# Moving 64 partition-group copies of the first mixer from ScalarE and VectorE to DMA, and some of its side products one main block later

## The chip, the cores and the metric

One core of one Trainium2 chip runs the whole program in a single launch. The core has five engines, each with its own instruction stream: TensorE (PE, matmuls into PSUM), VectorE (DVE), ScalarE (ACT), GpSimd (POOL) and SyncE (SP, which here issues DMAs). The metric is the device time of one launch in microseconds, the median of the runs.

## The reference

Two transformer blocks in fp32 over a sequence of 256 tokens, width 1024, batch 1. The first block puts 16 meta tokens ahead of the sequence (272 rows); the change touches only its mixer:

```python
hn = rmsnorm(h, norm1_g)
u, q, k, v, g_ssm, g_att = split(hn @ w_in)           # widths 512, 512, 512, 512, 1024, 1024
y_ssm = s5_mixer(u, ...)      # 32 groups of 16 channels, each a 64-dim complex state; scan over time
                              # y = gelu(Re(C s) + d * u);  y * sigmoid(y @ glu_w + glu_b)
q, k = rmsnorm per head ...
o = diff_attention(q, k, v, lam, slopes)               # 4 heads, softmax minus lam * softmax, ALiBi
y_att = rmsnorm(o, subln_g) * (1 - lam_init)
mixed = sigmoid(g_ssm) * (y_ssm @ w_ssm_out) + sigmoid(g_att) * (y_att @ w_att_out)
h = h + mixed @ w_o
h = h + conv_glu_ffn(rmsnorm(h, norm2_g), ...)
```

The second block (RG-LRU, HGRN2 and block-sparse attention side by side, then a squared-ReLU FFN and a final norm) is the same before and after.

## The kernel before

**Main work.** All large products keep fp32 accuracy by splitting both factors into a high and a low part of the faster fp32r type: `ah`/`al` for activations, `whi`/`wlo` for weights. A weight chunk of 1 MB is loaded by an SP DMA into one of two `raw` buffers (L109); ACT then makes `whi` (L133) and DVE makes `wlo` = raw - whi (L134). Half a chunk is a unit, which serves two blocks of 128 output rows (one for the first norm's direct products). A main block is 24 products, hi·hi, hi·lo and lo·hi for each of 8 slices of the contraction, into one of three `mm` PSUM tiles. `blocks()` walks units and blocks: in the first mixer the order is k, q (first norm's part in plain fp32), u (4 blocks), v (4), the 16 gate blocks `tg` (units 8 to 23), and then the output products of attention, the S5 gate, S5 and `w_o`. The next unit's split is issued after each block by `tick()`, up to four units ahead.

**Side work.** The S5 branch and the attention are Python generators. After each main block `bg.step()` advances them, by a budget of estimated DVE time, so that their small instructions are placed between the main blocks. After that a scheduler fixes the order on each engine; on the chip every engine runs its list in order and waits on semaphores. Side products use four `ps` PSUM tiles, and one `pso` tile for the attention's last norm. An instruction on PE that waits for ACT or DVE holds up all PE work behind it.

**The S5 branch.** Its preparation (`s5_prep`) forms small products of B and C (`s5cp`, `s5b`: 32 products), evicts them as `s5ks` (ACT), and copies them into the block-Toeplitz matrix `s5tz`: 16 copies of 32 partitions, each from one group of 32 partitions to another (`move`, L242 on ACT). It transposes `s5bp` by 32 PE transposes into 8 PSUM tiles, evicted as `s5lt` (ACT). When the u blocks are done, `stack()` copies `u` into `us`, 16 copies of 32 partitions x 272, so that time steps lie in partition groups. `s5_main` then goes through four channel tiles `ct`: 8 products with `s5lt`, eviction to `s5wk`, rotation, eight scans and rotation back on DVE (`s5wk`, `s5e`), 12 products with `s5cp` and `s5tz`, and eviction of the result `ys` into `us`. After the second and the fourth tile 16 copies of 32 x 136 bring the result back into `u` (`u<-us`): on ACT after the second (L242), on DVE after the fourth (L247), as the table `UNV = (1,)` says. A gelu (`u<-u`, ACT) and the split `yhl` follow.

**The attention.** The row norms of q and k run as a chain of small DVE instructions on `rw`, then ACT writes `rowt`, which PE spreads over the partitions (`rowt,bs`). Each head makes scores (`kraw,qz`), a softmax on DVE and ACT (`sc`, `sm`), five transposes of `sc`, an eviction to `wt`, and products `wt,vn`. After four heads the same chain on `rw` norms the result, `ya` is formed and split into `oh`/`ol`, the factors of the output product. A weight load on SP waits for the `wlo` that last read its raw buffer, and each engine's queue is served in order.

Of the kernel before, what the change touches and what calls it, by code (L numbers as in the profile page):

```python
# [33 lines left out]
NC = T // 4  # L34
# [19 lines left out]
MIX = "agass"  # L54
UNV, TZV, STV = (1,), (), ()
L_SO, L_O, L_F1, L_M2, L_F2 = 2, 0, 0, 2, 2
# [87 lines left out]


class Bg:


    def __init__(self, b):
        self.b, self.tc, self.tasks, self.ahead = b, b.tc, [], {}  # L150
        self.due = 0.0

    def add(self, gen, ahead=0):
# [4 lines left out]
    def one(self):  # L158
        for g in list(self.tasks):
            try:  # L160
                with self.tc.high_priority(self.ahead[g]) if self.ahead[g] else nullcontext():
                    self.b.side = True
                    next(g)
            except StopIteration:
                self.tasks.remove(g)
            self.b.side = False
# [12 lines left out]
    def finish(self, *gens):  # L179
        for g in gens:  # L180
            while g in self.tasks:
                self.one()


class Build:
    def __init__(self, ctx, tc, I, out, dbg):
        self.ctx, self.tc, self.I, self.out, self.dbg = ctx, tc, I, out, dbg or {}
        nc = self.nc = tc.nc
        self.V, self.A, self.G, self.PE = nc.vector, nc.scalar, nc.gpsimd, nc.tensor
        self.dve, self.side = 0.0, False  # L190
        self.bg = Bg(self)
        self.led = {}
        pool = lambda n, bufs, **k: ctx.enter_context(tc.tile_pool(name=n, bufs=bufs, **k))
        self.const = pool("const", 1)
        self.act_p = pool("act", 1)
        self.pad(self.act_p, 0)
        self.raw_p = pool("raw", 2)
        self.pad(pool("pad1", 1), 1)
        self.spl_p = pool("spl", 4)
        self.tmp_p = pool("tmp", 3)  # L200
        self.mm_p = pool("mm", 3, space=PSUM)
        self.ps_p = pool("ps", 4, space=PSUM)
        self.pso_p = pool("pso", 1, space=PSUM)
        self.dram = pool("dram", 1, space=DRAM)
# [38 lines left out]

    def move(self, o, i, vector):
        if vector:
            self.count(o)
            return self.V.tensor_copy(o, i)  # L247
        return self.cp(o, i)

# [102 lines left out]
    def s5_prep(self):  # L352
# [128 lines left out]
        for n in range(5):  # L481
# [17 lines left out]
            yield  # L499
        self.s5_stage = 1  # L500

        pk = self.ps()
# [11 lines left out]
        yield  # L514

        tz = self.s5_t
        for q in range(4):
            for i in range(4):
                self.move(tz[32 * i:32 * i + 32, :, q, i:4], ks[32 * q:32 * q + 32, :, 0:4 - i], i in TZV)
            yield  # L520

# [16 lines left out]
        for ct in range(2):  # L538
            self.s5_phases(ct)
            yield  # L540

# [43 lines left out]
    def s5_main(self):  # L585
# [7 lines left out]
        for ct in range(4):  # L593
# [38 lines left out]
            if ct % 2 == 1:  # L632
                for q in range(4):
                    for j in range(4):
                        o, i = yb[32 * q:32 * q + 32, ct - 1:ct + 1, j * NC:(j + 1) * NC], ys[32 * j:32 * j + 32, ct - 1:ct + 1, q]
                        self.move(o, i, ct // 2 in UNV)
                    yield
# [113 lines left out]
    def att_norm(self):  # L751
# [11 lines left out]
        self.rows_norm(p, 16, T, 1.0 / 64, eps=EPS * EPS)  # L763
        yield
        self.gk = a.tile([P, 1], F32, name="gk")
# [70 lines left out]
    def att_head(self, h):  # L836
# [26 lines left out]
        for i, (cols, _) in enumerate(rng):  # L863
            self.act(sc[:, 1, cols], sc[:, 1, cols], AF.Copy, scale=sm[:, 3, 2 + i:3 + i])
            self.stt(sc[:, 0, cols], sc[:, 0, cols], sm[:, 3, i:i + 1], sc[:, 1, cols], ALU.mult, ALU.add)
        yield
        p0, p1 = self.ps(), self.ps()
# [9 lines left out]
        self.cp(wt, p1[:, 0:3 * P])  # L877
        yield
        po = self.ps()
# [10 lines left out]
    def att_main(self):  # L890
# [9 lines left out]
        while gens or live:  # L900
            if gens:
                live.append(gens.pop(0))
            for _ in range(3):
                for g in list(live):
                    try:
                        next(g)
                    except StopIteration:
                        live.remove(g)
                yield
        self.show("o", self.o)  # L910
        self.rows_norm(self.pso, 8, TQ, 1.0 / P, mult=2.0 * (1.0 - LAM0))
        yield
        self.oh, self.ol = (a.tile([P, 4, RS], F32R, name=n, tag=t)[:, :, 0:TQ] for n, t in (("oh", "qz0"), ("ol", "qz1")))
# [52 lines left out]
    def blocks(self, ids, ah, al, n, bud=None, whole=None):  # L966

        b = 0
        for u in ids:
# [3 lines left out]
            self.W.used = u  # L973
            for c in range(w[0].shape[2] // P):
                if c < len(begun):
                    o, done = begun[c]
# [13 lines left out]
    def mixer1(self):  # L990
        tc, bg = self.tc, self.bg
        with ExitStack() as es:
# [28 lines left out]
            while self.s5_stage < 1:  # L1021
                bg.one()
            at = bg.add(self.att_main(), A_AT)
# [5 lines left out]
            def stack():  # L1029
                for q in range(4):  # L1030
                    for j in range(4):
                        self.move(self.us[32 * j:32 * j + 32, 0:16 * NC].rearrange("p (c q k) -> p c q k", c=4, q=4)[:, :, q],
                                  self.u[32 * q:32 * q + 32, :, j * NC:(j + 1) * NC], j in STV)
                        if j % 2 == 1:
# [9 lines left out]
            while self.s5_stage < 2:  # L1044
                bg.one()
            tg = self.tg = self.at_p.tile([P, 16, TQ], F32, name="tg", tag="tg")
# [788 lines left out]
```

## Time and profile before

| | before |
|---|---|
| time, median of 3 runs | 726.87 us (726.18 to 729.63) |
| profiled execution's own time | 726.51 us |
| span of the profiled execution | 724.7 us |
| PE busy | 699.3 us (96%) |
| DVE busy | 559.4 us (77%) |
| ACT busy | 437.6 us (60%) |
| POOL busy | 24.3 us (3%) |
| share of the chain that ended last: PE, DVE, ACT | 81%, 9%, 6% |

The span runs from the first to the last instruction of the profiled execution; the 1.8 us between it and that execution's time lie outside. Busy time is the time in which an engine executes; PE's is that of matmuls. The first mixer takes about the first 225 us. A timeline row gives an instruction (or several alike in a row, "x16"), when it starts, how long it takes, and in brackets how long the engine idled before it and which instruction ended that wait.

### The profile page before, as it was taken

How to read it: one execution, taken by the hardware profiler on the slowest of the kernel's cores; microseconds unless marked ns; L12 is line 12 of the kernel's file. 1: busy time of each engine (PE TensorE's matmuls, PEld its weight loads, DVE VectorE, ACT ScalarE, POOL GpSimd, SP SyncE). 2: the span in 40 equal slices, each digit the busy share in tenths (PEclk: the TensorE clock that was granted, in tenths of full speed). 3: DMA queues.
4: the chain of work that ended last, by engine and by line, in shares of the span. 5: the costliest groups of instructions: out<-in, count | busy, mean ns of one | idle time of the engine just before them, and what ended most of it. 6: DMA issues, size and time to landing. Idle time of an engine off the chain costs nothing.

```text
span 724.7 us, 13692 instructions
## 1 busy us (share of the span) xinstructions
PE 699.3 (96%) x5346; PEld 656.6 (91%) x5346; DVE 559.4 (77%) x1267; ACT 437.6 (60%) x813; POOL 24.3 (3%) x74
## 2 busy tenths in 40 slices
PE   8998998999999999999999998999899999999995
PEld 5886897989999999999999998898799999988884
DVE  8996788988989998888656598997778777744543
ACT  7488548655666655555454487779467666633421
POOL 5020000000001000000000300000000000000000
PEclk9999999999999999999999999999999999999999
DMA  7551303135457555445556634332237565555531
GB/s 256 203 184 72 123 35 117 59 117 175 179 181 252 178 198 206 176 175 189 190 167 212 211 139 175 118 117 73 103 117 241 203 214 186 181 213 188 179 112 58
DMA packets 18225, 117.24 MB, mean 162 GB/s; under 512 B 2160, under 2 KB 2416, under 8 KB 5360
## 3 DMA queue, kind: packets, MB, share of 16 engines
q1 hardware_dynamic: 17136, 113.55, 44.9%
q0 software_dynamic: 448, 2.16, 0.9%
q8 instruction: 42, 0.69, 0.4%
q10 hardware_dynamic: 576, 0.65, 0.3%
q14 instruction: 23, 0.19, 0.1%
HBM read 115.30 MB, written 1.05 MB: 161 GB/s over the span
## 4 chain that ended last, share of the span: by engine, by line
PE 81%; DVE 9%; ACT 6%; DMA 2%; issue 1%; SPq 0%; ACTq 0%; DVEq 0%
PE mm L263 72%; PE ps L263 7%; PE ps L259 2%; DVE wlo L134 2%; DVE s5w L217 1%; DMA cst<-in_cst_dram 1%; ACT s5tz L242 1%; ACT whi L133 1%; DVE s5bc L217 1%; ACT us L242 1%; DMA raw<-in_w_up_dram 1%; PE pso L263 1%; DVE s5x L217 1%; DVE s5an L236 1%; ACT u L242 1%
## 5 line engine op out<-in xcount | busy, mean ns | idle before, releaser
L133 ACT ACTIVATE whi<-raw 128x1024 fp32r<-128x1024 f32 (+1 forms) x206 | 215.5, 1051 | 193.2 <-PE mm L263 168.8
L134 DVE TENSOR_TENSOR wlo<-raw,whi 128x1024 fp32r<-128x1024 f32 (+1 forms) x206 | 249.9, 1214 | 103.1 <-ACT whi L133 101.8
L263 PE MATMUL mm<-ah,whi 128*128 128x256 f32 (+2 forms) x992 | 281.2, 284 | 0.4 <-DVE a L217 0.4
L263 PE MATMUL mm<-al,whi 128*128 128x256 f32 (+2 forms) x992 | 279.9, 282 | 0.0
L263 PE MATMUL mm<-ah,wlo 128*128 128x256 f32 (+2 forms) x992 | 279.2, 282 | 0.0
L263 PEld LDWEIGHTS mm<-ah,whi 128*128 128x128 f32 x992 | 187.4, 189 | 2.2 <-issue 1.0
L263 PEld LDWEIGHTS mm<-al,whi 128*128 128x128 f32 x992 | 187.4, 189 | 1.6 <-issue 1.1
L263 PEld LDWEIGHTS mm<-ah,wlo 128*128 128x128 f32 x992 | 187.3, 189 | 0.5 <-issue 0.4
L263 PE MATMUL mm<-whi,f2h 128*128 128x512 f32 x128 | 49.8, 389 | 0.0
L263 PE MATMUL mm<-whi,f2l 128*128 128x512 f32 x128 | 49.8, 389 | 0.0
L263 PE MATMUL mm<-wlo,f2h 128*128 128x512 f32 x128 | 49.8, 389 | 0.0
L263 PE MATMUL mm<-fl,whi 128*128 128x256 f32 x176 | 48.6, 276 | 0.0
L263 PE MATMUL mm<-fh,wlo 128*128 128x256 f32 x176 | 48.6, 276 | 0.0
L263 PE MATMUL mm<-fh,whi 128*128 128x256 f32 x176 | 48.6, 276 | 0.0
L263 PEld LDWEIGHTS mm<-fh,whi 128*128 128x128 f32 x176 | 33.0, 188 | 0.0
L263 PEld LDWEIGHTS mm<-fl,whi 128*128 128x128 f32 x176 | 33.0, 188 | 0.0
L263 PEld LDWEIGHTS mm<-fh,wlo 128*128 128x128 f32 x176 | 33.0, 188 | 0.0
L263 PE MATMUL mm<-hT,whi 128*128 128x272 f32 (+1 forms) x128 | 29.5, 389 | 0.0
L263 PEld LDWEIGHTS mm<-hT,whi 128*128 128x128 f32 x128 | 23.9, 190 | 5.2 <-ACT hT L239 1.3
L263 PEld LDWEIGHTS mm<-whi,f2h 128*128 128x128 f32 x128 | 24.0, 188 | 5.0
L263 PEld LDWEIGHTS mm<-whi,f2l 128*128 128x128 f32 x128 | 24.0, 188 | 5.0
L263 PEld LDWEIGHTS mm<-wlo,f2h 128*128 128x128 f32 x128 | 24.0, 188 | 4.9
(411 smaller groups left out, 1098.9 us busy)
## 6 DMA issues: line engine op xcount, KB each, us to landing
raw<-in_w_ff_dram SPq DMA_DIRECT2D x32, 1024.0 KB, 4.8
raw<-in_w_in_dram SPq DMA_DIRECT2D x24, 1024.0 KB, 4.8
raw<-in_w_up_dram SPq DMA_DIRECT2D x22, 1024.0 KB, 4.8
raw<-in_w_down_dram SPq DMA_DIRECT2D x8, 1024.0 KB, 4.8
whi<-in_w_in_dram SPq DMA_DIRECT2D x8, 512.0 KB, 5.0
raw<-in_w_o_dram SPq DMA_DIRECT2D x4, 1024.0 KB, 4.8
raw<-in_w_out_dram SPq DMA_DIRECT2D x4, 1024.0 KB, 4.8
raw<-in_w_down_dram SPq DMA_DIRECT2D x4, 768.0 KB, 4.4
```

Source lines behind the costliest of these rows:

```text
L133: b.A.activation(out=hi[:, 0:m], in_=raw, func=AF.Copy)
L134: b.V.tensor_tensor(out=lo[:, 0:m], in0=raw, in1=hi[:, 0:m].bitcast(F32), op=ALU.subtract)
L217: return self.V.tensor_tensor(out=o, in0=a, in1=b, op=op)
L236: return self.V.scalar_tensor_tensor(out=o, in0=a, scalar=s, in1=b, op0=op0, op1=op1)
L242: return self.A.activation(out=o, in_=i, func=AF.Copy)
L259: return self.PE.transpose(out=o, in_=i, identity=self.ident[0:k, 0:k])
L263: return self.PE.matmul(out=o, lhsT=l, rhs=r, start=start, stop=stop)
```

## The change

The three kinds of copy between partition groups become DMAs that SP issues, from SBUF to SBUF; the table `UNV` and the choice between ACT and DVE go. The 16 copies into `s5tz` are also issued later, after the transposes and the first phases of `s5_prep`. And a generator can now yield a mark, `LATER`, at six places: it is then not advanced again until the next main block has begun (`nblk`), whatever the budget. The marks stand before the `s5cp,s5b` products and before the `s5bp` transposes, after the row norm of q and k, in each head before the transposes of `sc` and before the products with `wt`, and after the last row norm. Where the program must have a generator's result, `force()` lifts the hold.

```diff
-UNV, TZV, STV = (1,), (), ()
...
+LATER = object()
...
     def one(self):
         for g in list(self.tasks):
+            if self.held.get(g) == self.b.nblk:
+                continue
             try:
...
-                    next(g)
+                    if next(g) is LATER:
+                        self.held[g] = self.b.nblk
...
-                self.one()
+                self.force()
+
+    def force(self):
+        self.held.clear()
+        self.one()
...
-    def move(self, o, i, vector):
-        if vector:
-            self.count(o)
-            return self.V.tensor_copy(o, i)
-        return self.cp(o, i)
+    def move(self, o, i):
+
+        self.nc.sync.dma_start(out=o, in_=i)
...
         self.s5_stage = 1
+        yield LATER
...
-        tz = self.s5_t
-        for q in range(4):
-            for i in range(4):
-                self.move(tz[32 * i:32 * i + 32, :, q, i:4], ks[32 * q:32 * q + 32, :, 0:4 - i], i in TZV)
-            yield
+        yield LATER
...
         for ct in range(2):
             self.s5_phases(ct)
+            yield
+
+        tz = self.s5_t
+        for q in range(4):
+            for i in range(4):
+                self.move(tz[32 * i:32 * i + 32, :, q, i:4], ks[32 * q:32 * q + 32, :, 0:4 - i])
             yield
...
-                        self.move(o, i, ct // 2 in UNV)
+                        self.move(o, i)
...
         self.rows_norm(p, 16, T, 1.0 / 64, eps=EPS * EPS)
-        yield
+        yield LATER
...
             self.stt(sc[:, 0, cols], sc[:, 0, cols], sm[:, 3, i:i + 1], sc[:, 1, cols], ALU.mult, ALU.add)
-        yield
+        yield LATER
...
         self.cp(wt, p1[:, 0:3 * P])
-        yield
+        yield LATER
...
             for _ in range(3):
+                wait = None
                 for g in list(live):
                     try:
-                        next(g)
+                        if next(g) is LATER:
+                            wait = LATER
...
-                yield
+                yield wait
...
         self.rows_norm(self.pso, 8, TQ, 1.0 / P, mult=2.0 * (1.0 - LAM0))
-        yield
+        yield LATER
...
             for c in range(w[0].shape[2] // P):
+                self.nblk += 1
```

On ACT, at the end of the S5 preparation, the order before is this (`s5lt` evicts the transposes, `sqa` are squares for the row norm, `vt` evicts v):

```order
L242 ACTIVATE s5tz<-s5ks 32x4x128
L242 ACTIVATE s5tz<-s5ks 32x4x96
L242 ACTIVATE s5tz<-s5ks 32x4x64
L242 ACTIVATE s5tz<-s5ks 32x4x32
L242 ACTIVATE s5lt<-ps 128x512 x5
L239 ACTIVATE sqa<-qraw 128x272 x2
L133 ACTIVATE whi<-raw 128x1024
L239 ACTIVATE sqa<-qraw 128x272
L242 ACTIVATE us<-u 32x4x68 x8
L242 ACTIVATE vt<-mm 128x272
L242 ACTIVATE us<-u 32x4x68 x4
L133 ACTIVATE whi<-raw 128x1024
```
and with the change it is this:

```order
L132 ACTIVATE whi<-raw 128x1024
L254 ACTIVATE s5bp<-s5bc 64x32x16 x2
L254 ACTIVATE s5ks<-ps 128x512
L254 ACTIVATE s5lt<-ps 128x512 x8
L251 ACTIVATE sqa<-qraw 128x272 x3
L132 ACTIVATE whi<-raw 128x1024
L254 ACTIVATE rowt<-rw 16x272
L254 ACTIVATE vt<-mm 128x272
L132 ACTIVATE whi<-raw 128x1024 x2
L254 ACTIVATE vt<-mm 128x272 x2
```
The copies into `s5tz` and `us` are gone from between the evictions, the eight `s5lt` evictions stand in one piece, and the three squares follow them at once. On PE the 32 transposes, which stood as 28 and 4 with 41 main products between, stand in a row too, with the eight `sqa` products right behind them and then 43 main products.

On DVE, in the first two channel tiles of the scan, the order before is this (`s5wk`, `s5e`: rotation and scan; the long-named `ISA` rows read scores; `wlo`: a weight unit's low half):

```order
L217 TENSOR_TENSOR s5wk<-s5wk 128x272 x2
L611 SCALAR_TENSOR_TENSOR s5wk<-mag_310,s5wk 128x68 x8
L851 ISA sc,sm<-ps,cst 128x272
L851 ISA sm 128x1
L217 TENSOR_TENSOR s5wk<-s5wk,s5e 128x2x4x68
L217 TENSOR_TENSOR s5wk<-s5wk,s5e 128x2x272
L231 TENSOR_SCALAR sm<-sm 128x4
L134 TENSOR_TENSOR wlo<-raw,whi 128x1024
L217 TENSOR_TENSOR s5wk<-s5wk 128x4x68 x2
L217 TENSOR_TENSOR s5e<-s5tt 128x288
```
and with the change this:

```order
L229 TENSOR_TENSOR s5wk<-s5wk 128x272 x2
L623 SCALAR_TENSOR_TENSOR s5wk<-mag_310,s5wk 128x68 x8
L243 TENSOR_SCALAR sm<-sm 128x4
L133 TENSOR_TENSOR wlo<-raw,whi 128x1024
L229 TENSOR_TENSOR s5wk<-s5wk,s5e 128x2x4x68
L229 TENSOR_TENSOR s5wk<-s5wk,s5e 128x2x272
L133 TENSOR_TENSOR wlo<-raw,whi 128x1024
L229 TENSOR_TENSOR s5wk<-s5wk 128x4x68 x2
L229 TENSOR_TENSOR s5e<-s5tt 128x288
L229 TENSOR_TENSOR s5wk<-s5tt 128x288
```
Both show the second tile's scan and what follows. Before, the `wlo` in it is that of unit 13, and unit 12's stood ahead of the first tile's chain; now the two that stand here are those of units 12 and 13.

On SP, from the third weight load of the gate blocks on, the order before is only loads:

```order
L125 DMA whi<-in_w_in_dram 128x1024
L109 DMA raw<-in_w_in_dram 128x2048 x10
L109 DMA raw<-in_w_att_out_dram 128x2048
L109 DMA raw<-in_ssm_glu_w_dram 128x2048
L109 DMA raw<-in_w_att_out_dram 128x2048
L109 DMA raw<-in_w_ssm_out_dram 128x2048 x2
```
and with the change the moves stand between them (ahead of these rows, behind three of the loads, stand the other 15 into `s5tz`):

```order
L258 DMA s5tz<-s5ks 32x4x32
L258 DMA us<-u 32x4x68 x12
L108 DMA raw<-in_w_in_dram 128x2048
L258 DMA us<-u 32x4x68 x4
L108 DMA raw<-in_w_in_dram 128x2048 x3
L258 DMA u<-us 32x2x68 x16
L108 DMA raw<-in_w_in_dram 128x2048 x3
L258 DMA u<-us 32x2x68 x16
L108 DMA raw<-in_w_att_out_dram 128x2048
```
A load that stands behind a move is issued when the move's own waits are over: those for `u` (DVE) for the moves into `us`, and those for the eviction of `ys` (ACT) for the moves into `u`. The gelu on ACT waits for the last of these. At the end of the attention, the eight `rowt,bs` products on PE, which stood as 1, 1, 2, 2 and 2 with main products between, now stand in a row, right ahead of the first products with `oh` and `ol`, behind 61 main products.

## Rows read from the trace of the kernel before

**Rows 1.** the page's first part: busy us (share of the span) xinstructions

```profile
PE 699.3 (96%) x5346; PEld 656.6 (91%) x5346; DVE 559.4 (77%) x1267; ACT 437.6 (60%) x813; POOL 24.3 (3%) x74
```

**Rows 2.** PE timeline: start us, us, instruction, [idle before <-releaser]

```profile
63.68 1.09 PE L259 MATMUL ps<-ident,s5bp 128*128 128x128 f32 x4 [2.27 <-ACT s5lt L242]
...
76.22 0.77 PE L263 MATMUL ps<-rowt,bs 128*128 128x272 f32 x4 [1.18 <-ACT rowt L242]
...
116.17 0.39 PE L259 MATMUL ps<-ident,sc 128*16 128x128 f32 x2 [0.98 <-DVE sc L236]
...
158.37 0.39 PE L263 MATMUL ps<-rowt,bs 128*128 128x258 f32 x1 [1.65 <-ACT rowt L242]
```

**Rows 3.** windows: stretch, us, busy us (x) PE, PEld, DVE, ACT, POOL, granted clock, DMA, GB/s

```profile
63.57:66.99 3.42, 3.31 (x12) 2.33 (x13) 2.63 (x15) 1.99 (x5) 0.00 (x0) 0.50 0.00 0
100.00:110.00 10.00, 10.00 (x79) 9.69 (x79) 10.00 (x32) 4.30 (x12) 0.00 (x0) 1.00 0.01 2
113.00:125.00 12.00, 9.99 (x67) 7.85 (x66) 8.41 (x33) 11.54 (x38) 0.00 (x0) 1.00 0.36 122
```

**Rows 4.** ACT timeline, 55 to 79 us, columns as in the PE timeline

```profile
55.25 7.67 ACT L242 ACTIVATE s5tz<-s5ks 32x512 f32<-32x512 f32 x16
...
62.94 2.56 ACT L242 ACTIVATE s5lt<-ps 128x512 f32<-128x512 f32 x5
...
69.10 3.49 ACT L242 ACTIVATE us<-u 32x272 f32<-32x272 f32 x8
```

**Rows 5.** instructions that touch u: xcount, ns min/median/max, first and last start

```profile
L242 ACT ACTIVATE us<-u x16: 413/428/434, 69.1 to 77.8; 32x272 f32<-32x272 f32 x16
L242 ACT ACTIVATE u<-us x16: 312/314/317, 113.5 to 122.2; 32x136 f32<-32x136 f32 x16
L247 DVE COPY u<-us x16: 219/222/227, 149.4 to 159.7; 32x136 f32<-32x136 f32 x16
```

**Rows 6.** DVE timeline, 94 to 110 us, around a weight unit's low half

```profile
94.65 1.36 DVE L217 TENSOR_TENSOR s5wk<-s5wk,s5e 128x544 f32<-128x544 f32 x2 [1.92 <-ACT s5wk L242]
...
108.48 1.22 DVE L134 TENSOR_TENSOR wlo<-raw,whi 128x1024 fp32r<-128x1024 f32 x1
```

**Rows 7.** PE timeline, 92 to 115 us: side products and two main products

```profile
92.26 1.92 PE L263 MATMUL ps<-us,s5lt 128*128 128x96 f32 x16
...
96.81 0.66 PE L263 MATMUL ps<-kraw,qz 128*128 128x144 f32 x4
...
100.75 0.58 PE L263 MATMUL ps<-s5wk,s5cp 128*128 128x96 f32 x4
...
114.79 0.29 PE L263 MATMUL mm<-ah,wlo 128*128 128x258 f32 x1
114.91 0.28 PE L263 MATMUL mm<-ah,whi 128*128 128x258 f32 x1
```

**Rows 8.** DVE timeline, 151 to 161 us: the attention's last norm

```profile
151.28 0.41 DVE L232 TENSOR_SCALAR rw<-pso 8x258 f32<-8x258 f32 x1
...
158.82 0.41 DVE L217 TENSOR_TENSOR rowt<-rw,rowt 8x258 fp32r<-8x258 f32 x1
...
160.00 0.48 DVE L236 SCALAR_TENSOR_TENSOR ya<-o,pk,ps 128x258 f32<-128x258 f32 x1
```

**Rows 9.** DMA issues on SP, start and us

```profile
5.76 0.63 SPq L649 DMA_DIRECT2D cst<-in_cst_dram  x1
...
155.50 0.33 SPq L109 DMA_DIRECT2D raw<-in_w_att_out_dram  x1
```

**Rows 10.** DMA issues on POOL, xcount, busy us, mean ns

```profile
L1052 POOL DMA_DIRECT2D hT<-in_hx_dram x1 | 0.7, 676 | 7.9 <-issue 7.9
```

**Rows 11.** DMA issues: xcount, KB each, median us to landing

```profile
raw<-in_w_in_dram SPq DMA_DIRECT2D x24, 1024.0 KB, 4.8
...
out_dram<-xg SPq DMA_DIRECT2D x2, 256.0 KB, 2.0
...
pk<-in_pk_dram ACTq DMA_DIRECT2D x1, 99.0 KB, 3.4
```

## What the change is predicted to do

> **What bounds the kernel now.** The page's first part comes first: PE is busy 699.3 of 724.7 us, DVE 559.4, ACT 437.6 [rows 1]. PE sets the end, so a copy that leaves ACT or DVE saves nothing by itself; it saves what PE stood idle for because of it. Next the PE timeline, for rows with a bracket in the first mixer. Four of them lie where the copies are [rows 2]: 2.27 us at 63.68, ended by an `s5lt` eviction; 1.18 at 76.22, ended by `rowt`; 0.98 at 116.17; 1.65 at 158.37, again `rowt`. The reader is to see in each that the engine named as releaser was late because of what stood ahead of it in its own queue. For the first the ACT timeline shows that: the 16 copies into `s5tz` run from 55.25 for 7.67 us, and the five evictions for which PE waits start only at 62.94 [rows 4]. The windows then give two things [rows 3]. From 63.57 to 66.99 the granted clock is 0.50, that is 1.2 instead of 2.4 GHz, right behind the idle 2.27 us; and from 113 to 125 PE is busy for 9.99 of 12 us. From 100 to 110 DVE is busy for all 10.00 us: there the S5 scan runs, and DVE has no room.
>
> **What goes.** All 64 copies leave: 16 of about 7.67/16 = 0.48 us [rows 4], 16 of 0.43 and 16 of 0.31 on ACT, 16 of 0.22 on DVE [rows 5], some 19.5 us of ACT and 3.6 of DVE. On the path that is:
> - At 63.68 the eight evictions now stand in one piece. Five take 2.56 us, 0.51 each [rows 4], about the pace of four transposes, so the 2.27 us go. With them should go the half clock, 3.42 us of which half, 1.7, is loss.
> - At 76.22 the `rowt` wait: the norm's DVE chain then has 43 main products beside it, which at 0.13 us each (0.12 for 258 columns [rows 7], times 272/258) is 5.5 us. I leave 0.4 of the 1.18 us, so 0.8 go. Bounds: none to all of it.
> - From 113 to 125 the idle 12 − 9.99 = 2.0 us [rows 3], which lie among the 16 copies `u<-us` on ACT (113.5 to 122.2 [rows 5]); at 158.37 the 1.65 us, whose DVE chain was interleaved with the 16 copies on DVE (149.4 to 159.7 [rows 5]).
>
> Together 2.27 + 1.7 + 0.8 + 2.0 + 1.65 = 8.4 us.
>
> **What comes in its place.** PE reaches the gate blocks some 4.8 us earlier, but DVE's scan moves up only with its first input, and the order has changed on DVE.
> - *Unit 12's low half.* It stood ahead of the first channel tile's chain; now it stands in the second tile's scan, at the place where unit 13's stood. Before, that place came 108.48 − 94.65 = 13.83 us behind the chain's first instruction; less the pair of 1.36 us that now follows instead of leading, plus the `wlo` itself, 1.22, it ends 13.7 us behind the first instruction [rows 6], and that one starts about 0.45 us behind the tile's last `s5lt` product. PE's way from that product to the first one with unit 12's low half, by the new order: eight more `s5lt` products, 1.92 (16 records are 8 products); scores, 0.66; 33 main products, 4.0; two wide scores, 1.0; 12 products with `s5cp` and `s5tz`, 2.5 (0.58 for two, four times, and the `s5tz` between); scores, 1.6; three main products, 0.4 [rows 7]. That is 12.1 us. PE waits about 13.7 + 0.45 − 12.1 = 2.0, and up to 2.8 where products overlap; I take 2.4. The second tile's `s5cp` products then wait for DVE another 0.5. Sum 2.9, bounds 1.4 and 3.5.
> - *The heads, each a block later.* The marks put main products between an eviction and its reader, 22 times 0.12 = 2.6 us where there were seven; that covers ACT. But the first head's `wt` copy on DVE stands behind the third tile's chain, the second head's wide scores wait for a `ps` tile that ACT empties only behind a weight half, and a head's norm product stands right behind its square. I take 2.0, bounds 0 (all covered) and 2.6.
> - *The attention's end.* The last norm's chain ran 151.28 to 159.23, 7.95 us [rows 8], with eight of the copies inside (8 × 0.22 = 1.8); with one weight half more (1.22) it is 7.4, and 0.4 for `rowt` on ACT make 7.8, against 61 main products, 7.3. With the hand-over PE waits 1.1 (bounds 0.5 and 1.5). Then the eight `rowt` products, which were spread among main products, stand in a row, and the `oh`, `ol` products follow at once: four `ya` at 0.48 and four subtractions of about 0.42 on DVE, with the first `oh` between, are some 4 us, of which the first output block's own 12 products cover 1.45. I take 2.0 (1.0 and 3.0).
>
> Together 2.9 + 2.0 + 1.1 + 2.0 = 8.0 us.
>
> **The moves themselves.** No row shows a DMA within SBUF or one of this shape (32 partitions of two or four short rows). Issue: from below 0.33 us, a plain load on SP, and 0.63, the dearest on SP [rows 9]; 0.68 on POOL [rows 10]; if each of the four rows per partition cost an issue of its own, 4 × 0.33 = 1.3. I take 0.45, near the SP rows. Landing: 2.0 us for 256 KB to 4.8 for 1 MB [rows 11]; these are 35 KB and less, so 2 to 2.5. With 0.45 the 28 moves ahead of the first `s5lt` product with `us` are issued from about 55 to 68 and landed by 71; PE needs them at about 83. The last 16 moves into `u` start when ACT evicts the fourth tile, some 31 us behind the second tile's `s5cp` products, take 7.2 + 2.3, and ACT comes to the gelu some 44 us behind them: 3 us are left. So the moves cost nothing, and no gain comes from them either. What covers them is this room; gone, the price is that of the third rival.
>
> Sum: 726.5 (the profiled execution; the median of the runs shown is 726.87, so nothing is to be corrected) − 8.4 + 8.0 = **726.1 us, taken as 726.0**. With every new wait at its lower bound (1.4 + 0 + 0.5 + 1.0 = 2.9) and the whole 1.18 gone it is 726.5 − 8.8 + 2.9 = 720.6; with every one at its upper bound (10.6) and the `rowt` wait kept, 726.5 − 7.6 + 10.6 = 729.5.
>
> **Rivals.**
> - *The front gain is kept.* The weight half and the heads do not hold PE, since ACT has 19.5 us more room: left are only the attention's end and half of the first wait, 3.1 + 1.2: 726.5 − 8.4 + 4.3 = 722.4, and 719.3 if the end too is covered. For it: every removed wait has a plain cause in the rows. Against it: DVE loses only 3.6 us of work, and it is full from 100 to 110 [rows 3].
> - *The clock falls again.* The wait of 2.4 us for unit 12 is as long as the 2.27 after which the clock went to half for 3.42 us [rows 2, 3]; the 1.65 at 158.37 had no such consequence. If both this and the attention's end (3.1 us) are followed by it, 726.0 + 2 × 1.7 = 729.4; with the waits at their upper bounds, 732.9.
> - *The SP queue is late* (slower). If a move costs 1.0 us to issue, the last `u` moves take 16 + 2.3 us where 44 − 31 = 13 are there: the gelu and all of ACT behind it, weight halves and the end of the attention too, are 5 us late, and the weight loads behind the moves as well: 731. At 1.3, the `us` moves land at 55 + 28 × 1.3 + 2.3 = 94 against 83: 726 + 11 = 737. It decides from (13 − 2.3)/16 = 0.67 us a move on. Against it: no SP row is above 0.63. For it: the pattern is one that no row has.
>
> A rule speaks for the last. The Trainium skill's page "DMA: Bandwidth & Descriptors", section "Bandwidth", wants transfers of 1 MiB and more and holds those under 64 KB to be ruled by their descriptors; the `us` moves are 35 KB. By its section "Anatomy of one DMA", told of POOL's path, most of a fixed 2 us is the wait for the write's receipt, not set-up, which would leave the issue short: an estimate by that page is 2.1 us from issue to landing for each, overlapped, and then the sum stands. The trace agrees in so far as 256 KB landed in 2.0 us; on short rows no run here shows it.
>
> **How the numbers follow.** My forecast (within bounds, 723 to 729) 0.52; front gain kept 0.22; clock 0.13; SP queue 0.13. A difference of 0.5%, 3.6 us, is about what a measurement of this kernel tells from none. Faster by more than that: nearly all of the second and 0.06 of the forecast's lower end, 0.27. Slower: the SP case, two fifths of the clock case and 0.07 of the upper end, 0.25. Between: 0.48. The range 720.5 to 732 leaves out the best corner of the front case and the SP case above 1 us a move.
>
> **What would show it.** Right: no 2.27 us in front of the transposes and full clock there; PE waits for `wlo` near 103, about 2.4 us; the wait at `rowt` and a wait for `ol` near 172; move issues under 0.6 us on SP, landed 10 us before their readers. Wrong: no wait at `wlo` (then the front case), a gelu that waits for a DMA on `u`, or SP with moves of 1 us and late weight loads.

## The result, and the profile after

| | after | before, same chips |
|---|---|---|
| median (14 runs each) | 730.56 us (727.82 to 735.64) | 727.34 us (725.19 to 729.63) |
| ratio | 1.0053, interval 1.0033 to 1.0073 | |
| profiled execution | 729.79 us, span 728.0 | 726.51 us, span 724.7 |

The change makes the kernel half a per cent slower, 3.2 us. The forecast was 726.0 us, no difference that can be told; the time lies inside the range given, on the slower side.

The page's first part, as [rows 1], of after:

```profile
PE 702.5 (96%) x5346; PEld 660.4 (91%) x5346; DVE 556.1 (76%) x1251; ACT 419.0 (58%) x765; POOL 24.4 (3%) x74
```

ACT lost 18.6 us of work and DVE 3.3, about what the 64 copies promised (19.5 and 3.6). PE runs the same 5346 matmuls but is busy 3.2 us longer: matmuls became slower somewhere. The PE timeline of after, its rows with a bracket between 53 and 174 us and the two behind the last of them, answers to [rows 2]:

```profile
53.05 3.69 PE L269 MATMUL ps<-ident,s5bp 128*128 128x128 f32 x32 [0.71 <-ACT s5bp L254]
...
67.04 1.27 PE L273 MATMUL ps<-rowt,bs 128*128 128x272 f32 x8 [0.28 <-ACT rowt L254]
...
106.43 0.39 PE L273 MATMUL mm<-ah,wlo 128*128 128x258 f32 x1 [2.65 <-DVE wlo L133]
...
113.75 0.46 PE L273 MATMUL ps<-us,s5lt 128*128 128x96 f32 x2 [0.49 <-ACT us L254]
...
123.29 0.70 PE L273 MATMUL ps<-wt,vn 128*128 128x258 f32 x2 [0.39 <-DVE wt L888]
...
168.85 1.24 PE L273 MATMUL ps<-rowt,bs 128*128 128x258 f32 x8 [0.22 <-ACT rowt L254]
172.92 0.55 PE L273 MATMUL mm<-oh,whi 128*128 128x258 f32 x1 [2.84 <-ACT oh L254]
173.27 0.42 PE L273 MATMUL mm<-ol,whi 128*128 128x258 f32 x1
173.49 0.42 PE L273 MATMUL mm<-oh,wlo 128*128 128x258 f32 x1
```

The transposes now stand in one row of 32 without the 2.27 us, and the `rowt` wait shrank to 0.28. New are 2.65 us for unit 12's low half and 2.84 for the last `oh`. The main products behind the second start every 0.22 us (173.27, 173.49) where [rows 7] had 0.12. The windows, columns as in [rows 3], say why:

```profile
63.57:66.99 3.42, 3.18 (x26) 2.96 (x24) 2.92 (x6) 1.23 (x3) 0.00 (x0) 1.00 0.25 54
106.00:107.00 1.00, 0.57 (x3) 0.57 (x4) 1.00 (x3) 1.00 (x5) 0.00 (x0) 0.87 0.02 8
107.00:110.00 3.00, 3.00 (x15) 3.00 (x15) 3.00 (x7) 0.21 (x2) 0.00 (x0) 0.50 0.19 22
110.00:111.00 1.00, 1.00 (x11) 1.00 (x9) 1.00 (x4) 0.00 (x0) 0.00 (x0) 0.93 0.60 172
170.00:171.00 1.00, 0.08 (x1) 0.00 (x0) 1.00 (x4) 0.72 (x2) 0.00 (x0) 1.00 0.00 0
171.00:172.00 1.00, 0.00 (x0) 0.00 (x0) 1.00 (x5) 0.49 (x2) 0.00 (x0) 0.79 0.00 0
172.00:178.00 6.00, 5.08 (x23) 5.11 (x24) 3.34 (x8) 1.51 (x4) 0.00 (x0) 0.50 0.28 101
178.00:179.00 1.00, 1.00 (x8) 1.00 (x8) 0.42 (x1) 0.71 (x1) 0.00 (x0) 0.79 1.01 426
```

The granted clock after the wait is the number that counts: 0.50 (1.2 of 2.4 GHz) from about 106.75 to 110.1 and from about 171.6 to 178.4. Three us at half clock hold 15 matmuls, one at full clock 11. The first stretch of 3.4 us loses 1.7, half of it; of the second, 5.5 us lie behind 172.92, where PE works again, and lose 2.7. The stretch of before at 63.57 is gone, its clock is 1.00.

The moves, by the instructions that touch `us` and `u` and the DMA issues of after, answer to [rows 5, 9, 11]:

```profile
L258 SPq DMA_DIRECT2D u<-us x32: 586/595/1077, 113.7 to 152.6; - x32
L258 SPq DMA_DIRECT2D us<-u x16: 585/600/652, 66.0 to 76.4; - x16
...
L251 ACT ACTIVATE u<-u x1: 1112/1112/1112, 157.5 to 157.5; 128x1088 f32<-128x1088 f32 x1
```

```profile
us<-u SPq DMA_DIRECT2D x16, 34.0 KB, 1.9
u<-us SPq DMA_DIRECT2D x32, 17.0 KB, 1.8
...
s5tz<-s5ks SPq DMA_DIRECT2D x4, 64.0 KB, 2.5
```

One move costs SP 0.60 us and lands, in the median of its kind, 1.8 to 2.5 us after its issue. No row of PE, ACT or DVE names one as what it waited for.

### The profile page after: what moved, and what is told of

The parts are those of the page before. It is cut to its first block, busy times and chain, and to the rows that moved or that the text cites. A ratio compares the mean times of both kernels' runs of the same rounds, so it can differ in the third digit from the quotient of the medians.

```text
span 728.0 us, 13731 instructions
## 1 busy us (share of the span) xinstructions
PE 702.5 (96%) x5346; PEld 660.4 (91%) x5346; DVE 556.1 (76%) x1251; ACT 419.0 (58%) x765; POOL 24.4 (3%) x74
## 4 chain that ended last, share of the span: by engine, by line
PE 76%; DVE 16%; ACT 3%; DMA 2%; issue 2%; SPq 0%; ACTq 0%; DVEq 0%
PE mm L273 68%; PE ps L273 6%; DVE wlo L133 3%; PE ps L269 1%; DVE s5wk L229 1%; DVE s5w L229 1%; DMA cst<-in_cst_dram 1%; DVE s5bc L229 1%; ACT whi L132 1%; PE pso L273 1%; DMA raw<-in_w_o_dram 1%; DVE s5x L229 1%; DVE s5wk L623 1%; DVE s5an L248 1%; DMA pk<-in_pk_dram 0%
```

## The experiments

Medians with their range; the ratio is to the kernel before, run on the same chip.

| run | median, us | ratio (95% interval) |
|---|---|---|
| marks_only | 727.12 (725.70 to 728.25) | 0.9998 (0.9984 to 1.0012) |
| moves_only | 722.82 (720.74 to 730.43) | 0.9958 (0.9930 to 0.9985) |
| fill | 727.18 (725.58 to 733.05) | 1.0015 (0.9987 to 1.0044) |
| moves_wlo_first | 726.14 (722.31 to 728.29) | 0.9988 (0.9968 to 1.0008) |
| no_last_mark | 732.97 (730.01 to 738.05) | 1.0101 (1.0067 to 1.0135) |
| tz_only | 722.53 (721.46 to 730.31) | 0.9964 (0.9941 to 0.9987) |
| moves_pool | 737.99 (737.05 to 738.43) | 1.0161 (1.0141 to 1.0180) |
| no_head_marks | 721.16 (719.21 to 727.15) | 0.9948 (0.9923 to 0.9972) |
| head_marks_only | 732.55 (730.71 to 737.77) | 1.0110 (1.0072 to 1.0148) |
| moves_fill | 721.52 (721.40 to 723.10) | 0.9940 (0.9922 to 0.9958) |
| moves_fill_again | 721.77 (719.10 to 724.30) | 0.9937 (0.9918 to 0.9957) |

**The two halves of the change apart.** marks_only is before with the six marks (copies left on ACT and DVE); moves_only is after with four of the marks a plain step, as here, and the two in the S5 preparation taken out:

```diff
-        yield LATER
+        yield
```

> The kernel before with the six marks LATER, and the moves left on ACT and DVE. Theory 1: the front is that of before (2.27 us idle behind the 16 s5tz copies, half clock behind it); in the end's order the rowt products stand before 30 main products, so no wait for oh appears: 726 to 728 us. Rival (holding side products back a block is by itself what costs): 730 us or more, with new waits in the heads between 110 and 160 us.

> The 64 moves as DMAs, with the mark LATER turned back into a plain yield at all places. Theory 1 (the moves are harmless and bring the front's gain; the loss at the attention's end comes from the marks, which gather the eight rowt products right ahead of the oh products): the wait for wlo of unit 12 (2.65 us) and the half clock behind it stay, the wait for oh (2.84 us) and the 5.5 us of half-clock products behind it (2.7 us) go, so 730.6 - 5.5 = 725.1 us. Rival (the moves on SP, 0.60 us each, hold up weight loads or ACT): no better than the changed kernel, 730 us, with waits for DMAs on ACT or DVE.

The moves alone make the kernel faster, the marks alone change nothing that can be told, and together they are slower than either: the loss is an interaction. In moves_only the wait for `oh` is gone; the one for unit 12 is not. Its median is 2.3 us below the 725.1 that was expected.

A median holds the whole program; the traces also tell where the first mixer ends. The first main product with 256 columns stands in the FFN right behind it. In the PE timelines of before, after and moves_only, in this order:

```profile
231.17 0.28 PE L263 MATMUL mm<-ah,whi 128*128 128x256 f32 x1
```

```profile
234.86 0.29 PE L273 MATMUL mm<-ah,whi 128*128 128x256 f32 x1
```

```profile
226.43 0.28 PE L273 MATMUL mm<-ah,whi 128*128 128x256 f32 x1
```

The change makes the mixer 3.7 us longer, the moves alone make it 4.7 us shorter. In marks_only it ends at 231.08, as before.

**Which of the moves.** tz_only is before with only the 16 `s5tz` copies as DMAs, issued behind the first phases.

```diff
-        tz = self.s5_t
-        for q in range(4):
-            for i in range(4):
-                self.move(tz[32 * i:32 * i + 32, :, q, i:4], ks[32 * q:32 * q + 32, :, 0:4 - i], i in TZV)
-            yield
...
+        tz = self.s5_t
+        for q in range(4):
+            for i in range(4):
+                self.nc.sync.dma_start(out=tz[32 * i:32 * i + 32, :, q, i:4], in_=ks[32 * q:32 * q + 32, :, 0:4 - i])
+            yield
```

> The kernel before with the 16 moves into s5tz alone as DMAs, issued where the change issues them; the other 48 stay on ACT and DVE, no marks. Theory 1 (the front's gain is that of these 16 copies, which stood ahead of the s5lt evictions): the 2.27 us in front of the transposes and the half clock behind it go, 4.0 us, and the waits at 116 to 122 and at the last rowt may stay or move: 726.9 - 4 = 723. Rival (the gain needs the other 48 off ACT as well): 725 to 727, with the rowt wait of about 1.2 us behind the us copies grown.

These 16 bring most of the gain. By the medians there is no difference to all 64 (0.9964 against 0.9958), but the intervals are wide. In the PE timeline of tz_only waits remain at places where moves_only has none over 0.3 us, and though it lacks the one of 2.65 us its mixer ends at 228.32, 1.9 us later than in moves_only:

```profile
111.17 0.43 PE L259 MATMUL ps<-ident,sc 128*16 128x128 f32 x2 [1.90 <-DVE sc L236]
...
154.44 0.39 PE L263 MATMUL ps<-rowt,bs 128*128 128x258 f32 x1 [1.45 <-ACT rowt L242]
...
228.32 0.28 PE L263 MATMUL mm<-ah,whi 128*128 128x256 f32 x1
```

The edit does two things, it makes the 16 copies DMAs and issues them later. No run issued them later and left them on ACT, so which of the two removes the 2.27 us was not shown.

**The clock.** fill leaves the changed kernel's order as it is, but for two score products that now stand ahead of two main ones, and puts products that nobody reads, into `pso`, where PE stood: 21 ahead of unit 12's block and 22 ahead of the first output block. The inputs come no earlier than in after; PE only does something meanwhile.

```diff
+                    if fill and b == 0:
+                        for k in range(fill):
+                            self.mm(self.pso[:, 0:TQ], w[0][:, k % w[0].shape[1], 0:P], self.ah[:, k % 8, T0:T])
```

> The changed kernel with 21 and 22 more products on PE (weights and activations that are there, into a PSUM tile whose content is not used), put into the wait for wlo of unit 12 and into the wait for oh; all else in the same order. They add nothing to the result. Theory 1 (each wait is followed by a stretch at half clock because PE stood idle, and those stretches cost 1.7 and 2.7 us on top of the idle time): PE works through both waits, the granted clock stays 1.0 there, and the time falls by 4.4 us to 726.2. Rival (the half clock has another cause than PE's idle time, as DVE or DMA load): the clock falls as in the changed kernel and the time stays 730.6, or rises by what of the products reaches beyond the waits, up to 0.5 us.

The PE timeline of fill at both places:

```profile
103.99 2.04 PE L273 MATMUL pso<-ah,whi 128*128 128x258 f32 x14
105.87 0.29 PE L273 MATMUL mm<-ah,whi 128*128 128x258 f32 x1
105.99 0.28 PE L273 MATMUL mm<-al,whi 128*128 128x258 f32 x1
106.40 0.39 PE L273 MATMUL mm<-ah,wlo 128*128 128x258 f32 x1
...
168.68 2.44 PE L273 MATMUL pso<-ah,whi 128*128 128x258 f32 x19
171.57 0.36 PE L273 MATMUL mm<-oh,whi 128*128 128x258 f32 x1 [0.44 <-ACT oh L254]
171.76 0.28 PE L273 MATMUL mm<-ol,whi 128*128 128x258 f32 x1
171.88 0.28 PE L273 MATMUL mm<-oh,wlo 128*128 128x258 f32 x1
```

The windows of fill, columns as in [rows 3], in the two stretches that after ran at half clock, and the first 256-column product:

```profile
107.00:110.00 3.00, 3.00 (x26) 2.88 (x25) 3.00 (x6) 0.17 (x2) 0.00 (x0) 1.00 0.22 27
172.00:178.00 6.00, 6.00 (x52) 6.00 (x51) 4.28 (x8) 2.15 (x4) 0.00 (x0) 1.00 0.50 173
```

```profile
230.56 0.28 PE L273 MATMUL mm<-ah,whi 128*128 128x256 f32 x1
```

The first product with unit 12's low half starts at 106.40, as in after (106.43), so nothing came earlier. But the output products now start every 0.12 us, and with 43 products more the mixer ends 4.3 us earlier than in after (234.86 − 230.56): 1.35 of them are there by the first product with `oh` (172.92 − 171.57), the rest comes behind it. That is the 4.4 us that the half clock was held to cost. DVE and ACT run the same instructions in the same order in both. The medians say the same less sharply: 727.18 against 730.56, with ratios whose intervals overlap a little, and five of fill's eleven runs took 729.7 us or more, of which no profile tells why.

**The wait for unit 12.** moves_wlo_first is moves_only with weight halves given priority over side work.

```diff
-A_PE, A_TK = 0, 0
+A_PE, A_TK = 0, 60
```

> The moves without the marks, and the weight halves scheduled with a priority of 60 instructions, which puts unit 12's wlo on DVE behind the first channel tile's scan instead of behind the second's. Theory 1 (PE waited for that one instruction's place in DVE's order): the wait of 2.65 us and the 1.7 us of half clock behind it go, and against the moves without marks the time falls by 4.4 us, to 720.7. Rival (DVE is full there, so the wait only goes on to the next thing that needs DVE): a wait of 2 to 3 us in front of the second tile's s5cp products, the clock falls behind it, and the time is that of the moves without marks, 725.

The wait for `wlo` went, and others took its place, as its PE timeline shows:

```profile
106.99 0.73 PE L273 MATMUL ps<-kraw,qz 128*128 128x272 f32 x2 [1.11 <-DVE sm L861]
...
108.62 0.73 PE L273 MATMUL ps<-kraw,qz 128*128 128x272 f32 x2 [0.91 <-DVE sm L861]
```

The DVE queue is full there, as [rows 3] had it from 100 to 110; a weight half put in front makes the softmax late. No half clock follows these waits. The first mixer ends no earlier than in moves_only (226.63 against 226.43; it began its transposes 1.1 us later), and the median is no better. Its profile has one loss of another kind: a wait of 2.29 us at 232.86, where the two weight loads issued between 220 and 232 us took 7.1 us in the median to land. tz_only's profile has 2.78 us there, the others 0.3 to 1.1. It lies behind what the change touches; whether it widens the spread of the runs was not shown.

moves_pool tries the rest of the room: moves_only with the rotation factors (`s5e`) of channel tiles 3 and 4 formed on GpSimd.

```diff
+        if ct < 2:
...
+            tt = self.tt
+        else:
...
+            tt = lambda o, x, y, op: self.G.tensor_tensor(out=o, in0=x, in1=y, op=op)
```

> The moves without the marks, with the six small products per tile that form the rotation of the third and fourth tile (s5e from s5tt) on GpSimd instead of DVE, 12 instructions, 4.4 us of DVE between the first tile's scan and unit 12's wlo and behind it. Theory 1 (PE waits for wlo of unit 12 because DVE has too much ahead of it): the scheduler puts the wlo right behind the first tile's chain, the wait of 2.65 us and its half clock, 1.7, go, and the time falls from 722.8 to 718.5. Rival (DVE is full until the second tile's s5cp products whatever stands where, or GpSimd's instructions are so slow that the third tile waits for them): a wait of 1 to 3 us in front of s5cp products, 721 to 724.

It fails: the kernel is 1.6% slower than before, beyond what the rival gave too. POOL timeline of moves_pool:

```profile
98.42 4.45 POOL L565 TENSOR_TENSOR s5e<-s5tt 128x288 f32<-128x288 f32 x2 [3.86 <-DVE s5wk L229]
102.83 1.75 POOL L565 TENSOR_TENSOR s5e<-s5e,s5w 128x288 f32<-128x288 f32 x2
```

What DVE does in 0.45 us took POOL 0.9 to 2.2 each, as far as its spans can be trusted. Waits of 1.49, 1.66 and 1.79 us appeared on PE at 97, 106 and 126, and 6.8 us of half clock from 109. The mixer ends at 233.89, 7.5 us later than in moves_only. The rest of the loss lies behind the mixer, where nothing was edited, and its cause stays open (see the end).

**Which mark.** Three runs. no_last_mark is after with the mark behind the last norm plain; no_head_marks has the two in `att_head` plain; head_marks_only has those two and no others. (The edit is always the one line above.)

> The changed kernel with the last of the six marks, the one behind the attention's last row norm, turned back into a plain yield; the rowt products then stand ahead of 24 main products instead of ahead of the oh products. Theory 1 (this mark makes the wait for oh, 2.84 us, and the half clock behind it, 2.7 us): both go, the wait for wlo with its half clock stays, 730.6 - 5.5 = 725.1 us. Rival (the wait for oh comes from the late heads, as the other marks make them, so 24 products of 0.12 us do not cover it): the chain behind the last norm is still late, 728 us or more.

> The changed kernel with the two marks in the heads (ahead of the scores' transposes and of the second wt transposes) plain again; the marks in front, in att_norm and ahead of the output product stay. Theory: the two marks in the heads push the heads' softmax chain and so the last norm back, and the end's late chain (0.5 + 2.84 us of waits and 2.7 us of half clock) comes from them; the products then stand as in moves_only, so the time is 722 to 725 us, with no wait over 1 us after 165 us and no half clock there. Rival: the marks of att_norm and of the output product alone bring the wait for oh; then 727.5 us or more, with a wait of 2 to 3 us near 172 us.

> The moves as DMA with only the two marks in the heads, the other four marks plain. Theory: the two head marks make the last row norm late, so the time is 730 to 734 us, as no_last_mark's 732.97: a wait for rowt of 2 to 3 us near 168 us, another for the output's chain near 173 us, and some 7 us or more at half clock there. Rival: without the marks in front and att_norm the heads have slack, and the time is 723 to 727 us with waits under 1.5 us at the attention's end.

My theory for no_last_mark fell: without that mark the kernel got slower still. PE timeline of no_last_mark:

```profile
168.62 1.98 PE L273 MATMUL ps<-rowt,bs 128*128 128x258 f32 x8 [2.93 <-ACT rowt L254]
...
173.07 0.58 PE L273 MATMUL mm<-ah,whi 128*128 128x258 f32 x1 [2.46 <-DVE z L229]
```

The last mark decides on which side of the last main block the first wait stands; ahead of that block it costs more. The marks in the heads decide that there is one: without them 721.16 (722 to 725 was expected), with them alone 732.55. The traces make this sharper. On every engine no_head_marks has, instruction for instruction, the order of moves_only, and head_marks_only that of no_last_mark: without the head marks the other four change nothing, and beside them only the last one does. The PE timelines show it by where the last head's norm product (`pso`) lies. Of before, after and no_head_marks, in this order:

```profile
148.85 0.60 PE L263 MATMUL pso<-sqo,cst 128*8 128x258 f32 x2
```

```profile
160.52 0.60 PE L273 MATMUL pso<-sqo,cst 128*8 128x258 f32 x2
```

```profile
144.53 0.60 PE L273 MATMUL pso<-sqo,cst 128*8 128x258 f32 x2
```

Behind it a norm chain of 7.7 us, `ya` and the split must run before the first output product, and PE has only the rest of the 704 main products that come before that one to fill the time. Counted in the timeline, 164 are left in before, 165 in no_head_marks and moves_only, 84 in marks_only, and 61 in after, head_marks_only and no_last_mark. 61 at 0.12 us are 7.3 us: they run out while the chain does. marks_only with 84 (10 us) is just covered, which is why the marks cost nothing there. The last head's product starts at nearly the same time in both, 160.04 in marks_only and 160.52 in after; with the moves PE has by then run 23 main products more, and so has fewer left. Why the order puts it there in both was not traced.

**The best of both.** moves_fill is moves_only with 21 products into the block's own tile ahead of unit 12's block (the block's first product then starts the sum anew).

```diff
+                    if b == 0:
+                        for k in range(fill):
+                            self.mm(o[:, 0:n], w[0][:, k % w[0].shape[1], 0:P], ah[:, k % 8])
```

> The moves without the marks, with 21 more products on PE, whose result is overwritten by the block's own first product, in the wait for wlo of unit 12. Theory 1: the wait itself is no shorter, but the granted clock stays 1.0 behind it, so 1.7 us less than the moves without marks: 721.1. Rival (the stretch at half clock costs nothing, because DVE is late in any case and the next thing from DVE is waited for instead): 722.8, with a wait of 1 to 2 us in front of the second tile's s5cp products.

> The same kernel as moves_fill (moves as DMA, no marks, 21 products into the block's own tile ahead of unit 12's block so that TensorE doesn't stand for wlo), beside the other two on one chip. Theory: 721 to 723 us, at or up to 2 us below no_head_marks, since the 2.65 us wait for wlo with 3.4 us at half clock behind it becomes 2.5 us of products. Rival: the earlier 721.52 was the spread of five runs and it is 724 us or more.

0.9940 and 0.9937 with intervals that exclude 1 by 0.4%: some 4.5 us faster than before, and by the ratios some 8 faster than the change. Against no_head_marks (721.16) there is no difference that can be told. The same stretch behind the same wait of 2.65 us explains that, in the windows of no_head_marks and then of moves_only:

```profile
107.00:110.00 3.00, 3.00 (x26) 2.88 (x25) 3.00 (x6) 0.18 (x2) 0.00 (x0) 1.00 0.19 22
```

```profile
107.00:110.00 3.00, 3.00 (x17) 3.00 (x16) 3.00 (x6) 0.19 (x2) 0.00 (x0) 0.54 0.17 22
```

One has 26 matmuls at clock 1.00, the other 17 at 0.54 (0.50 until 109.7), though all engines run the same instructions in the same order. head_marks_only and no_last_mark, the other such pair, differ here in the same way. So the half clock behind this wait is a matter of the execution: it came in three of five profiles with this wait (after, moves_only, no_last_mark), and in none of the three whose wait is filled (fill, moves_fill, moves_fill_again). Where it comes it costs 1.2 us by the mixer's end (226.43 against 225.21). The tops of the runs, 723.10 and 724.30 with the products against 727.15 and 730.43 without, are too far apart for that alone: of the 5.8 us by which moves_only's profiled execution (726.93) is longer than that of no_head_marks (721.16), 4.5 lie behind the mixer.

## Why the prediction was wrong, point by point

- *What goes*: right. 2.27, 1.7 of clock, 0.9 of the first `rowt` wait, 2.0 and 1.65 make 8.5 us (forecast 8.4); the 0.22 that is left of the last counts as a new wait below. The row of 32 transposes and the clock of 1.00 at 63.57 are what it had asked for. That the copies on ACT made the 2.0 us was not shown: of the three waits over 0.3 us there, DVE ended those of 0.98 and 0.44.
- *The moves*: the issue was 0.60 us, not 0.45, below the 0.67 from which the SP rival decides, and landing was 1.8 to 2.5 us in the median, as taken. By the fixed part that the Trainium skill's page "DMA: Bandwidth & Descriptors", section "Anatomy of one DMA", states, 2.1 us was the estimate for 35 KB; the trace agrees, with 1.9 us in the median for the moves into `us`. The last move into `u` starts at 152.6 and lands by 154.4, the gelu runs at 157.5: the 3 us of room that were forecast. The moves into `us` were to land by 71 and did so only at 81.7, since SP issued them every 0.65 us from 66.0 on, and the last four stood behind a 1 MB load issued at 73.80 and took 5.3 to 6.2 us. Their first reader starts at 82.3. "Landed 10 us before their readers" was wrong, and the step held by 0.6 us.
- *Unit 12*: right in mechanism and size. 2.65 us at 106.4 (forecast 2.4 near 103). The 0.5 behind it came at 113.75, but for ACT's `us` and not for DVE. The low half ends at 106.38, 13.8 us behind the tile's first DVE instruction (13.7):

```profile
92.56 1.36 DVE L229 TENSOR_TENSOR s5wk<-s5wk,s5e 128x544 f32<-128x544 f32 x2 [1.37 <-ACT s5wk L254]
...
105.16 1.22 DVE L133 TENSOR_TENSOR wlo<-raw,whi 128x1024 fp32r<-128x1024 f32 x1
```

- *The heads*: taken as 2.0 us of waits, measured 0.39. The price of the head marks was looked for inside the heads; it lies at the attention's end, to which they push the last norm.
- *The attention's end*: forecast 1.1 for `rowt` and 2.0 for `oh`; measured 0.22 and 2.84. The sum is right, the split not. The 2.0 counted on the first output block's products to run beside the last `oh`. They did not: the first of them starts at 172.92, when the fourth `oh` on ACT (172.47, 0.42) is done, and this fourth stands behind a fourth `ya` that DVE takes up only after three subtractions. DVE timeline of after:

```profile
169.76 1.27 DVE L248 SCALAR_TENSOR_TENSOR ya<-o,pk,ps 128x258 f32<-128x258 f32 x3 [0.52 <-PE ps L273]
170.95 1.10 DVE L229 TENSOR_TENSOR ol<-ya,oh 128x258 fp32r<-128x258 f32 x3
171.96 0.48 DVE L248 SCALAR_TENSOR_TENSOR ya<-o,pk,ps 128x258 f32<-128x258 f32 x1
```

- *The sum*: this step failed. New waits were forecast at 8.0 and measured at 2.65 + 0.49 + 0.39 + 0.22 + 2.84 = 6.6 us, so by waits alone the kernel would be 726.5 − 8.5 + 6.6 = 724.6. But each new wait was priced at its idle time only, though [rows 2, 3] had shown 1.7 us of loss behind one of 2.27, and the sum itself credits these 1.7 us where that wait goes. The half clock behind the new waits stood in it at nothing; it cost 1.7 and 2.7 us, which gives 729.0. The profiled execution took 729.79, and 0.8 us stay unassigned. fill bears this out: with the same arrivals and both waits worked through, the clock stays at 1.00 and the mixer ends 4.3 us earlier. The forecast missed by less than that because its waits were 1.4 us too high, which is luck.
- *The rivals*: "the clock falls again", at both places it named, is what happened, and its 729.4 us is the profiled execution's time within 0.4. It got 0.13 where by the rows it should have been the forecast: the sum held two waits of 2.4 and 3.1 us, and the only wait above 2 us in the rows had been followed by half clock. That the number fits so well is in part luck: it stood on waits 1.4 us too high, and its price of the clock was 1.0 too low, since the second stretch lasted 6.8 us and not 3.4. At unit 12 the half clock came in three of five profiles only.

One correction to the text ahead of the prediction: a unit serves two blocks only in the output products; in `w_in`, where the change lies, it serves one.

## What to carry to other kernels

When a trace has shown a wait of TensorE with half clock behind it, price each new wait of that length as its idle time plus such a stretch, and try products that nobody reads in its place before rebuilding the order. When side work is made later on purpose, count the main products left behind its last link and set them against the length of that chain: here 61 at 0.12 us against a chain put at 7.8 gave, ahead of any run, 3.1 us of waits where 3.06 came. Test the parts of a change apart, since here one part gains 4 us and the other turns that into a loss of 3.

## What the runs showed of the hardware

- A DMA from SBUF to SBUF, 32 partitions and 16 to 64 KB, occupied SP for 0.60 us and landed in 1.8 to 2.5 us in the median. In after, the four `us` moves behind the 1 MB load of 73.80 needed 5.3 to 6.2, and the first seven behind that of 141.50 needed 2.3 to 4.2.
- The half-clock stretches of the first mixer lasted 3.4 us in before, moves_only, marks_only, tz_only and at 107 of after and no_last_mark, but 6.8 us around the `oh` wait of after and 10.2 us around the waits of 2.93 and 2.46 us in no_last_mark and head_marks_only. Behind a wait of 1.90 us (tz_only, 111.17) it came; behind the same 2.65 us it came in three profiles of five, and behind waits of 1.45 (tz_only, 154.44), 1.49 (moves_pool, 97.13) and 1.65 us (before) it did not.
- In moves_only's profile the 256-column products from 240 to 420 us started every 117.8 ns instead of 113.3, at a granted clock of 1.00, some 4.6 us in all; of the other profiles moves_pool's alone has it, with 116 to 119 ns on the mean, and its cause stays open.
